# The second token half of x, also loaded transposed and scaled on chip, in one hybrid transformer layer

## The chip, the core and the metric

The kernel runs on one core of a Trainium2 chip. The core has a matrix engine, TensorE (PE; its weight loads are listed apart as PEld), three engines for elementwise work, VectorE (DVE), ScalarE (ACT) and GpSimd (POOL), and a queue engine, SyncE (SP), from which most transfers are issued. Each engine works through its own instruction stream; semaphores tie the streams together. The metric is the device time of one execution in microseconds.

## The reference

One layer is computed for 2048 tokens of width 1024, all in float32. The part that matters here is its beginning:

```python
u = rms_norm(h, g_mix_pre[l])          # x * rsqrt(mean(x*x) + eps) * g, per token
z = u @ w_in[l]                        # 1024 -> 2816 columns
qa, ka, va, qh, fh, ih, gh = jnp.split(z, IN_SPLITS, axis=-1)
```

The columns of z then feed a sliding-window attention (qa, ka, va) and a gated linear recurrence (qh, fh, ih, gh). For the recurrence the gate is f = lb + (1 - lb) sigmoid(fh), and running sums of log f over chunks of 64 tokens are exponentiated to give decays. Both outputs go through one projection, and cross-attention into 256 memory tokens and a SwiGLU network follow, each with its own norms.

## The kernel before

Every float32 operand of a matrix product is split into a high and a low part (`split2`), and a product is made of three matmuls, high by high, high by low and low by high (`products`, lines L1047, L1048 and L1049, which take turns). Large products are done in blocks with seven products in place of eight (`seven`); a block forms sums of weight tiles (`streamed`: sums at L1016, high parts at L911 on ScalarE or L913 on GpSimd, low parts at L914 on VectorE), multiplies, and copies banks of PSUM into `part` tiles on ScalarE (L1062) before it adds them up on VectorE (L571).

A planner in the framework orders the instructions of each engine ahead of time; the Python code is generators that the stage steps in turn, and a `yield` says how far a piece of work is moved behind the products. `behind()` ties an instruction to the last one of ScalarE and VectorE that `mark()` noted.

The first stage, `in_first`, lasts until about 268 us. It computes z for the first token half (1024 tokens) in eleven blocks of two 128-column groups, in the order `ORDER`: columns (4,5), (0,1), (2,3), then four forget-gate blocks (10+h, 6+h), then (14,15), (16,17), (18,19), (20,21). A block of the `seven` kind is 84 matmuls of 512 columns. Each has a closing generator, `after` in `in_block`. For a forget-gate block it runs `decays`: Ln (L652, with a table load before it and another before the next activation that needs the old table), two scans on VectorE (L656), small steps and a subtraction on GpSimd (L660, L661, L662, L665, L669), and exponentials on ScalarE (L668, L670, L672, L673). The gates themselves are tanh on ScalarE (L577) and a scale on GpSimd (L579); the other gates are L583 on ScalarE and L584 on VectorE.

Beside the blocks, the same stage prepares the second token half for the second stage. Block i gets some of the eight row tiles of x (`beside`): the tile is loaded on SP's queue into a `pair` tile when the block's weights are streamed; at the block's close `normed` squares it on ScalarE (L433), makes the factor 1/rms on GpSimd (`rstd`, L105 and L107) and scales the rows by factor and gain on VectorE (L435). After some yields eight transposes on TensorE (L1299) and two copies on ScalarE (L1300) turn it, and it is stored to a DRAM tile `un_d`. In the last blocks `fetch` loads `un_d` back in four pieces, and after all blocks the pieces are split into high and low parts (ScalarE L911, VectorE L914), ready for the second stage, whose first weights (`raw`) are split into `whi` on GpSimd (L148) and `wlo` on VectorE (L149), and whose first matmuls are L166, L167 and L168.

At the start of the stage the first half's own rows are squared, scaled and transposed too (L464, copies L470 on ScalarE, L481, L482), and the parts u of its second quarter are split on GpSimd (L913).

Of the kernel before, what the change touches and what calls it, by code (L numbers as in the profile page):

```python
# [24 lines left out]
KT = D // P  # L25
NFF = DFF // P
NB = 2
TB = T // NB
NPB = TB // P
# [19 lines left out]
class Layer:  # L49
# [27 lines left out]
    def store(self, dst, src):  # L77
        self.nc.sync.dma_start(dst, src)

    def put(self, dst, src):  # L80
        self.nc.scalar.dma_start(dst, src)

# [10 lines left out]
        self.load(g, ap[0:1, :].broadcast_to([P, D]))  # L93
        return g

    def rstd(self, parts, n, role):
# [9 lines left out]
        r = self.small(role + "_r")  # L106
        nc.gpsimd.tensor_tensor(r, v, self.mhalf[:, 0:1], ALU.pow)  # L107
        return r

# [61 lines left out]
    def run(self):  # L171
        tc, nc, I = self.tc, self.nc, self.I
        self._n = 0
        kw = dict(reuse_waits="tile")
        self.z_d = tc.dram_tile([DIN, T], F32, name="z_d")
        self.y_d = tc.dram_tile([NT, P, KT, P], F32, name="y_d")
        self.un_d = tc.dram_tile([KT, P, TB], F32, name="un_d")
# [247 lines left out]

    def pair_tile(self):
        self._n += 1
        return self.st_pool.tile([P, 2, D], F32, tag="pair", name=f"pair_{self._n}", bufs=5)

    def normed(self, x, junk):  # L430
        nc = self.nc
# [5 lines left out]
    def in_first(self):  # L437
# [59 lines left out]
                T[key[q, s]] = self.big.tile([P, 2, 4, 512], F32R, tag="big", name=f"u0_{q}{s}")  # L497
        second = {}

        def fetch():  # L500
            for s in range(2):
                for q in range(2):
                    r = self.pair_tile().rearrange("p a d -> p (a d)").rearrange("p (k t) -> p k t", k=4)
                    self.load(r, self.un_d[4 * q:4 * q + 4, :, s * 512:(s + 1) * 512].rearrange("k p t -> p k t"))
                    second[q, s] = r
                    yield

        beside = [(), (0,), (1, 2), (3,), (4,), (5,), (6,), (7,), (), (), ()]
        get = fetch()
        blocks = [("q" if i == 0 else "p" if i < 2 else "o",)  # L510
                  + self.in_block(*p, beside[i], get if i > 9 else (), None if i else lambda: x_loads(0, (2, 3)))
                  for i, p in enumerate(self.ORDER)]
        phases = self.phases([(lambda i, j, a, n: raw[i, j][:, a:a + n, :], 4, blocks, None, {})], T)
        next(phases)
        x_loads(1, range(4))
        b0 = first(0, "sh")
# [11 lines left out]
        self.mix_consts()  # L528
        for _ in phases:
            pass  # L530
        for _ in get:
            pass
        u = []
        for s in range(2):
            u.append([])
            for q in range(2):
                self._n += 1
                t = self.big.tile([P, 2, 4, 512], F32R, tag="big", name=f"u1_{q}{s}")
                r = second[q, s]
                for k in (0, 2):  # L540
                    self.split2(r[:, k:k + 2], t[:, 0, k:k + 2], t[:, 1, k:k + 2], "A")
                u[s] += [(t[:, 0, k, :], t[:, 1, k, :]) for k in range(4)]
        return u

    def in_block(self, ca, cb, beside, get, between):

        nc, w = self.nc, self.I["w_in"]
        z, x = [], []

        def load(t, j):  # L550
            if between and j:
                between()
            for i, c in enumerate((ca, cb)):
                self.load(t[:, i, :], w[c, :, j * 512:(j + 1) * 512])

        def stream(kind):
            for n in beside:
                t = self.pair_tile()
                self.load(t[:, 0, :], self.I["x"][TB + n * P:TB + (n + 1) * P, :])
                x.append((n, t))  # L560
            for _ in range(3):
                next(iter(get), None)
            return self.streamed(load, 4, kind, tiled=True)

        def out(i, j, a, b):
            if not z:
                z.append(self.pair_tile())
            c0 = (ca, cb)[i] * P
            zs = z[0][:, i, j * 512:(j + 1) * 512]
            if b is not None:  # L570
                nc.vector.tensor_tensor(zs, a, b, ALU.add)  # L571
                a = zs
            if c0 < C_QH or C_IH <= c0 < C_GH:
                if b is None:
                    nc.scalar.activation(zs, a, AF.Copy)
            elif C_FH <= c0 < C_IH:
                nc.scalar.activation(zs, a, AF.Tanh, scale=0.5)  # L577
                h = (c0 - C_FH) // P
                nc.gpsimd.tensor_scalar(zs, zs, self.fb[:, h:h + 1], self.fa[:, h:h + 1], ALU.mult, ALU.add)  # L579
            else:  # L580
                self._n += 1
                t = self.st_pool.tile([P, 512], F32, tag="part", name=f"th_{self._n}", bufs=self.parts)
                nc.scalar.activation(t, a, AF.Tanh, scale=0.5)  # L583
                nc.vector.scalar_tensor_tensor(zs, t, 1.0, a, ALU.add, ALU.mult)  # L584
# [63 lines left out]
    def decays(self, b, h, f, e1, e2):  # L648

        nc = self.nc  # L650
        NCB = TB // 64
        nc.scalar.activation(e1, f, AF.Ln)  # L652
        yield
        for s in range(TB // 512):
# [318 lines left out]
    @contextlib.contextmanager  # L973
    def behind(self):

        with contextlib.ExitStack() as at:
            for e in (mybir.EngineType.Activation, mybir.EngineType.DVE):
                if self.last.get(e) is not None:
                    at.enter_context(self.tc.issue_after(self.last[e]))
            yield  # L980

    def mark(self):

        traced = self.nc.cur_bb.bb.instructions
        self.last = {}
        for e in (mybir.EngineType.Activation, mybir.EngineType.DVE):
# [721 lines left out]
```

## Time and profile before

| | |
|---|---|
| median of 3 runs | 2575.55 us (2574.43 to 2576.95) |
| profiled execution | 2576.83 us |
| its span | 2574.7 us |
| TensorE busy | 2518.1 us, 98% |
| VectorE, ScalarE, GpSimd busy | 68%, 49%, 19% |
| matmuls on TensorE | 12160 recorded |

The span is the time between the first and the last instruction of the profiled execution. In the rows of the profile a line number such as L1299 is a line of the kernel, a group is written out<-in with the names of the program's tiles, and a bracket such as [0.93 <-POOL u L913] says how long the engine was idle before that instruction and what ended the wait. The waits of an engine are listed as total in us, number of times, longest. The clock column of the stretches is the share of TensorE's full clock that was granted.

### The profile page before, as it was taken

The page shows a single profiled execution, that of the slowest core. Times are in us where ns is not written, and L with a number is a line of the kernel's source. Part 1 is how long each engine was busy: PE and PEld are TensorE (multiplying, and loading weights), DVE is VectorE, ACT ScalarE, POOL GpSimd, SP SyncE. Part 2 cuts the span into 40 slices and gives each one's busy share as a digit, 9 for nine tenths or more (in the row PEclk, how much of TensorE's full clock was granted, in tenths as well). Part 3 has the DMA queues.
Part 4 walks back from the last instruction along what each step waited for, and adds up shares of the span by engine and source line. Part 5 has one row for each costly group of instructions (what it writes and reads, how often), then busy time and mean ns, then how long its engine had stood idle before and what let it go on. Part 6 is the DMA issues. An engine that isn't in the chain of part 4 may idle for free.

```text
span 2574.7 us, 34494 instructions
## 1 busy us (share of the span) xinstructions
PE 2518.1 (98%) x12160; PEld 2108.6 (82%) x12160; DVE 1747.3 (68%) x2781; ACT 1262.3 (49%) x2641; POOL 481.6 (19%) x651
## 2 busy tenths in 40 slices
PE   7989999999999999999999999999999999999998
PEld 6878788878997888888788888888888888888786
DVE  7675578778666668697776665575666566664756
ACT  5453366656555575565564333353333334543443
POOL 4240334321321334224210000000000000000022
PEclk9999999999999999999999999999999999999999
DMA  5335655484896787767983542253555434576798
GB/s 188 135 119 180 198 159 153 150 259 169 251 331 236 229 273 218 246 229 207 314 264 123 171 163 83 82 196 123 180 200 193 158 128 142 191 220 185 224 222 211
DMA packets 285389, 495.78 MB, mean 193 GB/s; under 512 B 20640, under 2 KB 143520, under 8 KB 285216
## 3 DMA queue, kind: packets, MB, share of 16 engines
q1 hardware_dynamic: 272256, 446.38, 51.5%
q0 software_dynamic: 10656, 38.80, 8.1%
q10 hardware_dynamic: 2304, 8.39, 0.8%
q8 instruction: 96, 1.57, 0.3%
q14 instruction: 77, 0.63, 0.1%
HBM read 326.78 MB, written 166.72 MB: 192 GB/s over the span
## 4 chain that ended last, share of the span: by engine, by line
PE 86%; DMA 5%; DVE 4%; issue 2%; POOL 2%; ACT 1%; SPq 0%; DVEq 0%; POOLq 0%; ACTq 0%
PE psm L1047 23%; PE psm L1049 23%; PE psm L1048 23%; PE psg L168 2%; PE psg L166 2%; PE psg L167 2%; PE pss L1299 2%; DMA pair<-in_x_dram 1%; PE pss L167 0%; PE psh L168 0%; PE psh L167 0%; PE pss L168 0%; PE pss L166 0%; PE psh L166 0%; DMA qd<-z_d 0%
## 5 line engine op out<-in xcount | busy, mean ns | idle before, releaser
L1047 PE MATMUL psm<-T,S 128*128 128x512 f32 x2664 | 1032.7, 392 | 14.9 <-ACT part L1062 8.6
L1048 PE MATMUL psm<-T,S 128*128 128x512 f32 x2664 | 1039.5, 390 | 0.0
L1049 PE MATMUL psm<-T,S 128*128 128x512 f32 x2664 | 1033.6, 391 | 2.2 <-DVE S L914 2.2
L1047 PEld LDWEIGHTS psm<-T,S 128*128 128x128 f32 x2664 | 501.1, 188 | 121.9 <-ACT part L1062 10.5
L1049 PEld LDWEIGHTS psm<-T,S 128*128 128x128 f32 x2664 | 500.9, 188 | 108.2 <-DVE S L914 4.4
L1048 PEld LDWEIGHTS psm<-T,S 128*128 128x128 f32 x2664 | 501.2, 188 | 102.6
L911 ACT ACTIVATE S<-sum 128x512 fp32r<-128x512 f32 (+1 forms) x338 | 207.9, 619 | 329.6 <-PE psm L1049 320.5
L914 DVE TENSOR_TENSOR S<-sraw,S 128x512 fp32r<-128x512 f32 (+1 forms) x311 | 214.8, 698 | 220.6 <-ACT S L911 208.3
L914 DVE TENSOR_TENSOR S<-sum,S 128x512 fp32r<-128x512 f32 (+1 forms) x404 | 277.1, 691 | 79.9 <-ACT S L911 67.0
L1062 ACT ACTIVATE part<-psm 128x512 f32<-128x512 f32 x297 | 175.3, 592 | 188.9 <-PE psm L1049 180.5
L911 ACT ACTIVATE S<-sraw 128x512 fp32r<-128x512 f32 (+1 forms) x272 | 166.4, 617 | 143.3 <-PE psm L1049 137.6
L1417 POOL DMA_DIRECT2D row<-y_d x28 | 25.0, 892 | 1071.4 <-DMA sraw<-hid_d 905.3
L1388 ACT ACTIVATE junk<-row 128x512 f32<-128x512 f32 x160 | 99.6, 624 | 95.3 <-DVE row L1410 34.6
L914 DVE TENSOR_TENSOR T<-row,T 128x1024 fp32r<-128x1024 f32 x104 | 123.3, 1193 | 29.6 <-ACT T L911 29.3
L166 PE MATMUL psg<-u,whi 128*128 128x512 f32 x352 | 141.8, 403 | 1.0 <-POOL whi L148 1.0
L168 PE MATMUL psg<-u,wlo 128*128 128x512 f32 x352 | 140.2, 398 | 1.5 <-DVE wlo L149 1.5
L167 PE MATMUL psg<-u,whi 128*128 128x512 f32 x352 | 140.1, 398 | 0.0
L911 ACT ACTIVATE T<-row 128x1024 fp32r<-128x1024 f32 x104 | 105.6, 1026 | 24.7 <-DMA row<-in_w_down_dram 11.8
L913 POOL TENSOR_SCALAR S<-sum 128x512 fp32r<-128x512 f32 x66 | 51.9, 787 | 217.8 <-PE psm L1049 138.6
L1592 DVE TENSOR_TENSOR part<-psm,part 128x512 f32<-128x512 f32 x66 | 45.5, 689 | 66.5 <-PE psm L1049 66.4
L149 DVE TENSOR_TENSOR wlo<-raw,whi 128x1024 fp32r<-128x1024 f32 x54 | 68.8, 1274 | 27.6 <-ACT whi L146 18.9
L1583 DVE TENSOR_TENSOR row<-psm,part 128x512 f32<-128x512 f32 x66 | 45.5, 690 | 56.0 <-PE psm L1049 55.7
(331 smaller groups left out, 3659.2 us busy)
## 6 DMA issues: line engine op xcount, KB each, us to landing
sraw<-in_w_gate_dram SPq DMA_DIRECT2D x44, 512.0 KB, 4.9
sraw<-in_w_up_dram SPq DMA_DIRECT2D x44, 512.0 KB, 4.8
hid_d<-row SPq DMA_DIRECT2D x44, 512.0 KB, 2.7
h_d<-row SPq DMA_DIRECT2D x32, 512.0 KB, 6.9
y_d<-row SPq DMA_DIRECT2D x32, 512.0 KB, 3.8
sraw<-hid_d SPq DMA_DIRECT2D x32, 512.0 KB, 5.2
row<-h_d POOLq DMA_DIRECT2D x30, 512.0 KB, 7.7
row<-y_d POOLq DMA_DIRECT2D x28, 512.0 KB, 7.2
```

Source lines behind the costliest of these rows:

```text
L149: nc.vector.tensor_tensor(lo, raw, f32(hi), ALU.subtract)
L166: nc.tensor.matmul(ps, ah, bh, start=(i == 0), stop=False)
L167: nc.tensor.matmul(ps, ah, bl, start=False, stop=False)
L168: nc.tensor.matmul(ps, al, bh, start=False, stop=(i == n - 1))
L911: self.nc.scalar.activation(hi, raw, AF.Copy)
L913: self.nc.gpsimd.tensor_scalar(hi, raw, 1.0, 1.0, ALU.mult, ALU.mult)
L914: self.nc.vector.tensor_tensor(lo, raw, f32(hi), ALU.subtract)
L1047: nc.tensor.matmul(ps, s[:, 0, k, :], t[:, 0, k, :], start=st, stop=False, **kw)
L1048: nc.tensor.matmul(ps, s[:, 0, k, :], t[:, 1, k, :], start=False, stop=False, **kw)
L1049: nc.tensor.matmul(ps, s[:, 1, k, :], t[:, 0, k, :], start=False, stop=sp, **kw)
L1062: nc.scalar.activation(t, ps, AF.Copy)
L1388: self.nc.scalar.activation(junk, a, AF.Square, scale=float(D) ** -0.5, accum_out=to)
```

## The change

Four things change, all in the first stage.

1. The host hands over the second half of x also transposed (`x_t`, four pieces of 1 MB) and the gain as columns (`g_mix_t`). `fetch` loads the pieces straight from there, from the eighth block on in program order, and not from `un_d`, which goes away with its stores, its row scaling (L435), its 64 transposes (L1299) and its copies (L1300).
2. The row tiles are still loaded and squared, to get the factors. They now go through a buffer of their own, `xr`, which exists once; the square overwrites the tile, and the factor goes to a column of `r_u`. The load is issued in the block's closing generator.
3. A new generator `scaled`, stepped beside the ninth block, spreads the factors: for each 512 tokens four transposes of a factor column broadcast to 128 x 128 give a PSUM bank whose every row holds the factors, and eight products on VectorE multiply pieces of `x_t` by gain column and bank, in place. A generator `parted`, beside the last block, splits the pieces into high and low parts. Both are tied with `behind()`, which now also holds an instruction behind the last one of TensorE.
4. `decays` has one more `yield` ahead of Ln, the other generators' yields change by one, `pair` tiles exist six times and not five, and the stores of z for columns from 18 on go out from GpSimd's queue (`store_late`).

```diff
+    def store_late(self, dst, src):
+        self.nc.gpsimd.dma_start(dst, src)
...
-        return self.st_pool.tile([P, 2, D], F32, tag="pair", name=f"pair_{self._n}", bufs=5)
+        return self.st_pool.tile([P, 2, D], F32, tag="pair", name=f"pair_{self._n}", bufs=6)
...
         def fetch():
+            self.load(g_t, I["g_mix_t"])
             for s in range(2):
                 for q in range(2):
...
-                    self.load(r, self.un_d[4 * q:4 * q + 4, :, s * 512:(s + 1) * 512].rearrange("k p t -> p k t"))
+                    self.load(r, I["x_t"][2 * s + q])
...
-        beside = [(), (0,), (1, 2), (3,), (4,), (5,), (6,), (7,), (), (), ()]
+        def scaled():
+            for s in range(2):
+                ps = self.bank("sh"[s])
+                with self.behind():
+                    for i in range(4):
+                        n = 4 * s + i
+                        nc.tensor.transpose(ps[:, i * P:(i + 1) * P], self.r_u[:, n:n + 1].broadcast_to([P, P]),
+                                            self.ident)
+                for q in range(2):
+                    r = second[q, s]
+                    for k in range(4):
+                        with self.behind():
+                            nc.vector.scalar_tensor_tensor(r[:, k, :], r[:, k, :], g_t[:, 4 * q + k:4 * q + k + 1],
+                                                           ps, ALU.mult, ALU.mult)
+                        yield
+
+        def parted():
+            for n in (1, 3, 2, 0):
+                for _ in range(n):
+                    yield
+                s, q = divmod(sum(map(len, u)) // 4, 2)
...
+                with self.behind() if n else contextlib.nullcontext():
+                    for k in (0, 2):
+                        self.split2(second[q, s][:, k:k + 2], t[:, 0, k:k + 2], t[:, 1, k:k + 2], "A")
+                u[s] += [(t[:, 0, k, :], t[:, 1, k, :]) for k in range(4)]
+
+        beside = [(), (0, 1), (2, 3), (4,), (5,), (6,), (7,), (), (), (), ()]
...
-                  + self.in_block(*p, beside[i], get if i > 9 else (), None if i else lambda: x_loads(0, (2, 3)))
+                  + self.in_block(*p, beside[i], get if i > 6 else (), None if i else lambda: x_loads(0, (2, 3)))
...
-        phases = self.phases([(lambda i, j, a, n: raw[i, j][:, a:a + n, :], 4, blocks, None, {})], T)
+        phases = self.phases([(lambda i, j, a, n: raw[i, j][:, a:a + n, :], 4, blocks, None, {8: [scaled], 10: [parted]})], T)
...
         def after():
-            for n, p in x:
-                self.normed(p[:, 0, :], p[:, 1, :])
+            def rows(n):
+                self._n += 1
+                t = self.st_pool.tile([P, D], F32, tag="xr", name=f"xr_{self._n}", bufs=1)
+                self.load(t, self.I["x"][TB + n * P:TB + (n + 1) * P, :])
+                return t
+
+            t = rows(beside[0]) if beside else None
...
-                self.store(self.z_d[c * P:(c + 1) * P, 0:TB], z[0][:, i, :])
-            for _ in range(1 if C_FH <= c0 < C_IH else 4):
-                yield
-            for n, p in x:
-                self.store_transposed(self.un_d, n, self.transposed(p[:, 0, :], p[:, 1, :]))
+                (self.store if c < 18 else self.store_late)(self.z_d[c * P:(c + 1) * P, 0:TB], z[0][:, i, :])
+            for _ in range(1 if C_FH <= c0 < C_IH else 3):
+                yield
+            for n in beside:
+                if n != beside[0]:
+                    t = rows(n)
+                    for _ in range(3):
+                        yield
+                ss = self.small("n_s")
+                nc.scalar.activation(t, t, AF.Square, accum_out=ss)
+                self.rstd([ss], D, "n", self.r_u[:, n:n + 1])
                 yield
...
         NCB = TB // 64
+        yield
         nc.scalar.activation(e1, f, AF.Ln)
...
-            for e in (mybir.EngineType.Activation, mybir.EngineType.DVE):
+            for e in (mybir.EngineType.Activation, mybir.EngineType.DVE, mybir.EngineType.PE):
```

In the planner's order that results, the eight squares all stand among ScalarE's instructions of the first 20 to 57 us of the old timeline, because nothing holds their loads back; of the eight transposes four stand within the first products of the ninth block and four in the tenth block.

More of the change, by code (lines that the diff above doesn't have):

```diff
@@ L94, in gain, with rstd @@
         return g
-    def rstd(self, parts, n, role):
+    def rstd(self, parts, n, role, r=None):
         nc = self.nc
@@ L105, in rstd @@
             nc.gpsimd.tensor_scalar(v, parts[0], 1.0 / n, EPS, ALU.mult, ALU.add)
-        r = self.small(role + "_r")
+        if r is None:
+            r = self.small(role + "_r")
         nc.gpsimd.tensor_tensor(r, v, self.mhalf[:, 0:1], ALU.pow)
@@ L176, in run @@
         self.y_d = tc.dram_tile([NT, P, KT, P], F32, name="y_d")
-        self.un_d = tc.dram_tile([KT, P, TB], F32, name="un_d")
         self.h1t_d = tc.dram_tile([NT, P, KT, P], F32, name="h1t_d")
@@ L498, in in_first @@
         second = {}
+        self.r_u = self.mc.tile([P, NPB], F32, name="r_u")
+        g_t = self.mc.tile([P, KT], F32, name="g_t")
+        u = [[], []]
         def fetch():
+            self.load(g_t, I["g_mix_t"])
             for s in range(2):
@@ new lines, in parted @@
+        def parted():
[4 more added lines that the diff above has]
+                self._n += 1
+                t = self.big.tile([P, 2, 4, 512], F32R, tag="big", name=f"u1_{q}{s}")
+                with self.behind() if n else contextlib.nullcontext():
+                    for k in (0, 2):
+                        self.split2(second[q, s][:, k:k + 2], t[:, 0, k:k + 2], t[:, 1, k:k + 2], "A")
+                u[s] += [(t[:, 0, k, :], t[:, 1, k, :]) for k in range(4)]
@@ L530, in in_first @@
             pass
[L531 to L542, printed above, removed]
         return u
@@ L547, in in_block @@
         nc, w = self.nc, self.I["w_in"]
-        z, x = [], []
+        z = []
         def load(t, j):
@@ L556, in stream @@
         def stream(kind):
[L557 to L561, printed above, removed]
+            for _ in range(2):
                 next(iter(get), None)
@@ L586, in after @@
         def after():
-            for n, p in x:
-                self.normed(p[:, 0, :], p[:, 1, :])
+            def rows(n):
+                self._n += 1
+                t = self.st_pool.tile([P, D], F32, tag="xr", name=f"xr_{self._n}", bufs=1)
+                self.load(t, self.I["x"][TB + n * P:TB + (n + 1) * P, :])
+                return t
+            t = rows(beside[0]) if beside else None
             c0 = ca * P
@@ L985, in mark @@
         self.last = {}
-        for e in (mybir.EngineType.Activation, mybir.EngineType.DVE):
+        for e in (mybir.EngineType.Activation, mybir.EngineType.DVE, mybir.EngineType.PE):
             self.last[e] = next((i for i in reversed(traced) if i.engine == e), None)
@@ L1699 @@
             host[name] = tiled(host[name].T if name == "wq_x" else host[name])
+    host["x_t"] = np.ascontiguousarray(host["x"][TB:].reshape(2, 512, 2, 4, P).transpose(0, 2, 4, 3, 1)).reshape(4, P, 4, 512)
+    host["g_mix_t"] = np.ascontiguousarray(host["g_mix_pre"].reshape(KT, P).T)
     nc = _bacc.Bacc("TRN2", target_bir_lowering=False, num_devices=1, dynamic_dma_scratch_size=2048)
```

## The prediction

> **What bounds the kernel now.** The page comes first: its busy shares and its costliest groups.
>
> ```profile
> PE 2518.1 (98%) x12160; PEld 2108.6 (82%) x12160; DVE 1747.3 (68%) x2781; ACT 1262.3 (49%) x2641; POOL 481.6 (19%) x651
> ...
> L1047 PE MATMUL psm<-T,S 128*128 128x512 f32 x2664 | 1032.7, 392 | 14.9 <-ACT part L1062 8.6
> ```
>
> TensorE is busy 98% of the span, so only two things can move the time: work taken off PE, and pauses of PE. The diff touches the first stage (0 to about 268 us), which alone holds nearly all of the 8.6 us that PE waited for L1062. The waits of PE there, then busy time by stretches, with the granted clock in the column after the five engines:
>
> ```profile
> PE psm L1047 <- ACT part L1062: 8.1, 4, 4.9
> ...
> PE psg L168 <- DVE wlo L149: 1.5, 1, 1.5
> PE psg L166 <- POOL whi L148: 1.0, 1, 1.0
> PE psm L1047 <- POOL u L913: 0.9, 1, 0.9
> PE psm L1047 <- ACT S L911: 0.8, 1, 0.8
> ```
>
> ```profile
> 20.00:40.00 20.00, 16.24 (x130) 14.83 (x130) 14.64 (x19) 12.09 (x24) 11.08 (x17) 1.00 0.20 73
> ...
> 120.00:140.00 20.00, 19.74 (x92) 16.17 (x90) 14.84 (x20) 11.68 (x19) 9.95 (x12) 1.00 0.50 159
> ...
> 160.00:180.00 20.00, 15.09 (x60) 12.07 (x60) 16.62 (x20) 12.88 (x20) 10.35 (x11) 0.83 0.42 149
> ...
> 260.00:280.00 20.00, 16.99 (x67) 13.05 (x66) 15.96 (x20) 6.46 (x10) 14.46 (x13) 0.91 0.90 297
> ```
>
> The four waits for L1062 stand at the starts of the forget-gate blocks (two of them long). In 160:180 the clock averages 0.83: 0.17 x 20 / 0.5 = 6.8 us at half clock, of which about 5.5 us lie after PE resumed, so 2.75 us more are lost there. In 260:280 it is 0.91: 3.6 us at half clock, 1.6 to 1.8 us lost. Who makes L1062 late is read from ScalarE's timeline (idle time before an instruction, and its releaser, in brackets) and from the chain of waits:
>
> ```profile
> 132.92 1.06 ACT L433 ACTIVATE pair<-pair 128x1024 f32<-128x1024 f32 x1 [4.27 <-DMA pair<-in_x_dram]
> ...
> 139.31 1.28 ACT L583 ACT_TABLE_LOAD   x1
> ...
> 157.55 1.06 ACT L433 ACTIVATE pair<-pair 128x1024 f32<-128x1024 f32 x1 [4.09 <-DMA pair<-in_x_dram]
> ...
> 163.40 1.06 ACT L652 ACTIVATE pair<-pair 128x1024 f32<-128x1024 f32 x1 [1.83 <-POOL pair L579]
> ```
>
> ```profile
> 119.51 0.50 PE L1047 MATMUL psm<-T,S 128*128 128x512 f32 x1 [0.74 <-ACT part L1062]
> ...
> 141.74 0.50 PE L1047 MATMUL psm<-T,S 128*128 128x512 f32 x1 [2.00 <-ACT part L1062]
> ...
> 166.90 0.80 PE L1047 MATMUL psm<-T,S 128*128 128x512 f32 x1 [4.91 <-ACT part L1062]
> ```
>
> ```profile
> 78.01 0.88 PE pss L1299 x8
> ...
> 126.89 5.95 DMA pair<-in_x_dram
> ...
> 150.48 6.99 DMA pair<-in_x_dram
> ...
> 201.64 0.45 PE psm L1047 x2
> ...
> 207.77 0.87 PE pss L1299 x8
> ```
>
> ScalarE works through its queue in order. The square of a row tile of x (L433) stands there ahead of the gate's activations; its load, 6 to 7 us long, came late; behind it came th, L577, the table load, Ln (after POOL's L579), a second table load, L583, and only then L1062, for which PE waited.
>
> **The change, part by part.**
>
> *Transposes.* Of eight sets of eight at L1299 seven lie on PE's path at 0.87 us (two are in the chain above). The first set, at 37.55 us, ends in the wait for POOL's u (the 0.9 row) and costs nothing. The new kernel has eight transposes in all, tied to PE's own order: 0.87. Net 7 x 0.87 - 0.87 = **5.2 us gained**. The two copies of each set and L435 leave ScalarE and VectorE; the sixteen new products of x, gain and factor go to VectorE:
>
> ```profile
> 119.94 0.68 DVE L584 SCALAR_TENSOR_TENSOR pair<-th,psm 128x512 f32<-128x512 f32 x1
> ```
>
> Sixteen at that price are 11 us, spread over blocks 8 to 10, about 60 us in which VectorE was busy some 10 us in 20. Costed at nothing; without that cover each of them ahead of a PE operand would cost up to 0.68.
>
> *Squares away from the gate blocks.* All eight now stand early (20 to 57 us). In the second gate block the square held ScalarE's queue for 4.27 + 1.06; without it L577 still has to await VectorE's sum, about 1.5 of that, so the second table load ends near 136.8 instead of 140.6 (139.31 + 1.28). PE paused at 139.74 there, and L583 and L1062 take 1.1: 2 us of slack. What stays is inherent: L583 reads the last product of the old block, then L1062 (0.5 + 0.6 us) frees a bank, and PE has only three matmuls of 0.227 (the 0.45 of two, above) between: 1.1 + 0.2 - 0.68, about 0.65 us a boundary, much as the first of the three waits (0.74) and the fourth of the table (8.1 - 0.74 - 2.00 - 4.91, about 0.5). At the last gate boundary the order moved differently: L670, L668, L672 and L673, which wait for POOL's L661 and L665, now stand ahead of L583 and L1062. Their timing at that place before:
>
> ```profile
> 180.65 1.06 ACT L652 ACTIVATE pair<-pair 128x1024 f32<-128x1024 f32 x1
> ...
> 189.00 1.06 ACT L670 ACTIVATE pair<-pair 128x1024 f32<-128x1024 f32 x1 [4.25 <-POOL pair L661]
> ...
> 192.11 1.07 ACT L1062 ACTIVATE part<-psm 128x512 f32<-128x512 f32 x2
> ```
>
> ```profile
> 181.44 0.69 DVE L1016 TENSOR_TENSOR sum<-sraw,sraw 128x512 f32<-128x512 f32 x1 [2.10 <-DMA sraw<-in_w_in_dram]
> ...
> 182.65 2.33 DVE L656 TENSOR_TENSOR_SCAN pair<-reset,pair 128x512 f32<-128x512 f32 x2
> ```
>
> ```profile
> 180.78 0.39 PE L1047 MATMUL psm<-u,S 128*128 128x512 f32 x1
> ```
>
> The scans will not stand behind a sum that waits for weights, as at 181.44, but follow Ln at 181.7: with what lay between scan and L670 (182.65 to 189.00, less a POOL product of 1.05) L670 starts about 187; the exponentials, L583 and L1062 take 4.2 more with POOL's last small steps: 191.3. PE, whose new order comes back to that bank 36 matmuls after the block's start (180.78 + 36 x 0.227 = 188.95), waits about **2.5 us**. Before: 0.74 + 2.00 + 4.91 + 2.75 (clock) + 0.84 (the wait for L911, at the last boundary) + a 0.2 next to it = 11.4. After: 3 x 0.65 + 2.5 = 4.45. **7.0 us gained.** Bounds: nothing waits at the last boundary, 9.5; or the 2.5 us pause also halves the clock as the 4.9 one did, 4.2.
>
> *The early squares.* They share one buffer, so load and square alternate, and each square stands in ScalarE's order among the copies L470 that feed the first 512-wide matmuls:
>
> ```profile
> 36.90 1.09 ACT L470 ACTIVATE pair<-pss 128x512 f32<-128x512 f32 x2 [0.26 <-PE pss L464]
> ```
>
> ```profile
> 39.62 0.96 PE L1047 MATMUL psm<-u,S 128*128 128x512 f32 x3 [0.93 <-POOL u L913]
> ```
>
> The price of a load: the one row tile loaded with little beside it took from 61.79 to about 65, the median of all eight is 5.6.
>
> ```profile
> 61.79 0.33 SPq L75 DMA_DIRECT2D pair<-in_x_dram  x1
> ...
> 65.08 1.06 ACT L433 ACTIVATE pair<-pair 128x1024 f32<-128x1024 f32 x1 [2.05 <-DMA pair<-in_x_dram]
> ```
>
> ```profile
> pair<-in_x_dram SPq DMA_DIRECT2D x8, 512.0 KB, 5.6
> ```
>
> In 20:40 the DMA share was 0.20 and SP's queue holds nothing but these loads (and one of g_mem), so I take 3.2 plus a square of 1.06. The second square can end about 30.7 (behind the copies of that time); the third then stands at 34.0 to 35.1, the fourth at 38.3 to 39.4, so the last copies move from 36.90 to 39.4; POOL's u follows, interleaved with two factors of r_u, and the first 512-wide matmul comes at about 41.5 instead of 39.62: **1.9 us lost**. PE has only sixteen transposes, 1.7 us, in the seven before 41.5. Around the stage's last pauses (1.0 and 1.5 us, a few matmuls between) the clock fell; here I expect the same, one stretch of that length, **1.7 lost**. Bounds 0 and 5: no delay, or two such stretches (3.4) with 1.6. The Trainium skill (TensorE: Matmul & The Clock Gate, "What's actually happening") says that the clock halves after an idle window of about 3.4 us, in windows that run freely. Read strictly, no such window would be quite idle here, the clock would hold and the time be 2564.3; this trace's 0.91 in 260:280 followed pauses with matmuls between, which speaks against the strict reading. The later squares delay copies that have 2 us and more to spare; costed at nothing. If the loads took 5.6, the fourth square would end at 45.6 instead of 39.4, and with two stretches at half clock 1.9 + 6.2 + 3.4 = 11.5 would be lost instead of 3.6.
>
> *The end of the stage.*
>
> ```profile
> 260.73 1.28 SPq L75 DMA_DIRECT2D raw<-in_w_in_dram  x3
> ...
> 264.15 1.40 POOL L148 TENSOR_SCALAR whi<-raw 128x1024 fp32r<-128x1024 f32 x1 [13.91 <-DMA raw<-in_w_in_dram]
> ...
> 264.57 2.13 DVE L584 SCALAR_TENSOR_TENSOR pair<-th,pair 128x512 f32<-128x512 f32 x2
> ...
> 266.62 1.21 DVE L149 TENSOR_TENSOR wlo<-raw,whi 128x1024 fp32r<-128x1024 f32 x1
> ```
>
> The raw load is still tied to the same matmul, 15 before the stage's last, so the pause of 1.0 for whi stays. The splits (parted) begin inside the last block, and L149 need not stand behind two L584: about **1.0 us gained**, between 0 (the raw load sets all) and 2.6 (the clock holds too). SP loses sixteen row transfers of x and un_d and gains eight earlier ones; the four x_t loads, as large as the four of un_d that they replace, go out three blocks before their use. The last four z_d stores move from SP to POOL's queue, nearest row:
>
> ```profile
> L1417 POOL DMA_DIRECT2D row<-y_d x28 | 25.0, 892 | 1071.4 <-DMA sraw<-hid_d 905.3
> ```
>
> Two of them (0.9 each) stand ahead of whi on POOL, but their data are ready some 10 us before: nothing, or at worst 1.8 late. The rest of the program keeps its order but for a few neighbours: 0.
>
> *Sum.* 5.2 + 7.0 - 3.6 + 1.0 = 9.6. The profiled execution took 2576.83 us (span 2574.7 and 2.1 around it), 1.28 above the median of 2575.55. 2576.83 - 9.6 = 2567.2; against the median 2565.95, so I forecast **2566 us**.
>
> **Rivals.**
>
> *Half of it comes back.* The 2.5 us pause halves the clock (2.75) and the early stretch costs 5: 5.2 + 4.2 - 5 + 0 = 4.4, 2571. For it: the page's 0.83 after one pause. Against it: the second L1062 pause of 2.00 us lies in 120:140, where the clock stayed at 1.00. Loads at 5.6 us would give 9.6 - 7.9 = 1.7, 2574, in the same class.
>
> *Slower: Ln goes on holding L1062 back.* Ln and its two table loads still stand ahead of L583 and L1062 at the other three boundaries. Were L579 or the scan's neighbours on POOL late there by more than the 2 us of slack, each would cost as the last: 2.5 + 2.75 instead of 0.65, 3 x 4.6 = 13.8, and 2.75 at the last: 9.6 - 16.6 = -7.0, 2582.5. It decides the sign from an average of about 2.5 us a boundary for all four. For it: the row at 163.40, where Ln waited 1.83 for L579. Against it: that L579 followed an L577 which the late square had pushed.
>
> *More.* The early copies hide the squares, the last boundary waits for nothing, the clock holds at the end: 5.2 + 9.5 + 0 + 2.6 = 17.3, 2558.
>
> *It does nothing at the end of the stage*: the raw load sets that end alone, 2567; it lies inside the forecast.
>
> **How the numbers follow.** A measurement here tells 0.2% (5.15 us) from no change: faster is under 2570.4, slower over 2580.7. Forecast (2562 to 2570.4) 0.50; more gain 0.15; half, contended loads included, 0.20; slower 0.10; 0.05 lies between half and slower. So faster 0.65, same 0.25, slower 0.10. The range 2559 to 2576 leaves out about 0.05 below and 0.13 above.
>
> **What would show it.** L1299 gone and eight transposes in its place; the L1062 waits in the first stage at about 4.5 us in four, none over 3, and the clock 1.00 in 160:180; the first 512-wide matmul at 41 to 42 us, with a clock under 1.00 in 20:60; L149's wait under 1. The prediction is wrong if PE waits for ScalarE at the gate boundaries as long as before, if the row loads take 5 us or more, or if new waits of PE on VectorE show in blocks 8 to 10.

## The result, and the profile after

The changed kernel takes 2581.25 us (median of 9 runs, 2579.5 to 2587.34) against 2576.3 us before: a ratio of 1.0021 [1.0012, 1.003]. It is 5 us slower, where 2566 us, 10 us faster, was forecast. The profiled execution took 2584.18 us with a span of 2582.4, 7.7 us above that of the kernel before.

Lines have moved, most by some thirty: L1047 is now L1079, L1062 is L1094, L1299 is L1331, L148 and L149 are L152 and L153, L166 to L168 are L170 to L172. First the page, the busy shares and the costliest group:

```profile
PE 2522.1 (98%) x12104; PEld 2103.4 (81%) x12104; DVE 1742.3 (67%) x2789; ACT 1256.5 (49%) x2625; POOL 471.4 (18%) x655
...
L1079 PE MATMUL psm<-T,S 128*128 128x512 f32 x2664 | 1031.7, 391 | 13.1 <-ACT S L943 5.8
```

56 fewer matmuls are recorded, and yet PE is busy 4.0 us longer (2518.1 before). That is the first sign that the loss is more than a new wait. The waits of PE in the first 300 us of the changed kernel:

```profile
PE psm L1079 <- ACT part L1094: 4.1, 5, 1.8
...
PE psm L1079 <- POOL u L945: 3.0, 1, 3.0
...
PE psg L170 <- ACT z L659: 1.6, 1, 1.6
PE psg L172 <- DVE wlo L153: 1.5, 1, 1.5
PE psg L170 <- POOL whi L152: 0.7, 1, 0.7
```

The wait for L1094 (L1062 before) halved, 8.1 to 4.1. Its pieces, the first 512-wide matmul and the first product of the next stage, from PE's timeline:

```profile
41.99 1.42 PE L1079 MATMUL psm<-u,S 128*128 128x512 f32 x3 [2.98 <-POOL u L945]
...
122.25 0.50 PE L1079 MATMUL psm<-T,S 128*128 128x512 f32 x1 [0.48 <-ACT part L1094]
...
142.66 0.50 PE L1079 MATMUL psm<-T,S 128*128 128x512 f32 x1 [0.71 <-ACT part L1094]
...
163.10 0.50 PE L1079 MATMUL psm<-T,S 128*128 128x512 f32 x1 [0.71 <-ACT part L1094]
...
184.97 0.50 PE L1079 MATMUL psm<-T,S 128*128 128x512 f32 x1 [1.75 <-ACT part L1094]
...
244.90 0.50 PE L1079 MATMUL psm<-T,S 128*128 128x512 f32 x1 [0.49 <-ACT part L1094]
...
260.41 0.50 PE L170 MATMUL psg<-u,whi 128*128 128x512 f32 x1 [0.71 <-POOL whi L152]
```

The same product of the kernel before:

```profile
265.61 0.50 PE L166 MATMUL psg<-u,whi 128*128 128x512 f32 x1 [1.04 <-POOL whi L148]
```

So the first stage, where all four terms of the forecast lie, ended 5.2 us earlier, and what follows it took 12.9 us longer than before. Part of that are waits late in the program, which the change doesn't touch. Behind 794 us PE waited for S:

```profile
PE psm L1079 <- ACT S L943: 5.8, 3, 2.5
PE psm L1081 <- DVE S L946: 4.9, 5, 1.5
```

Before, the same two were 3.7 and 2.2. A profile is one execution, and these waits differ between the profiles of all kernels below. The other part of the loss shows where PE waits for nothing. Two stretches of the second stage's first products without a pause, first and last row of each, before and after:

```profile
286.62 0.39 PE L168 MATMUL psg<-u,wlo 128*128 128x512 f32 x1
...
290.92 0.39 PE L166 MATMUL psg<-u,whi 128*128 128x512 f32 x1
```

```profile
282.74 0.39 PE L172 MATMUL psg<-u,wlo 128*128 128x512 f32 x1
...
286.94 0.40 PE L172 MATMUL psg<-u,wlo 128*128 128x512 f32 x1
```

Before, 19 steps took 4.30 us, 226 ns each; after, 18 steps took 4.20 us, 233 ns each: the same instruction, at full clock, 7 ns slower. (Over all steps of 215 to 245 ns between 260 and 500 us the mean goes from 229.1 to 233.4.) The first stage shows the same in the durations (minimum, median and maximum in ns, first and last start) of its products with u, before and after:

```profile
L1048 PE MATMUL psm<-u,S x125: 387/389/397, 60.2 to 257.1; 128*128 128x512 f32 x125
```

```profile
L1080 PE MATMUL psm<-u,S x132: 393/394/398, 60.4 to 255.6; 128*128 128x512 f32 x132
```

No instruction of these products was changed. What the change did alter is the place of their operands: `r_u` and `g_t`, two tiles of 32 bytes in each partition, come first in pool `mc`, and all tiles allocated behind them in it, among them the weights S, whi and wlo, moved by 64 bytes, while u stayed where it was in pool `big`. In the compiled programs' addresses, taken modulo 256 bytes, the moving and the stationary operand of a 512-wide product before had the same start in 9640 of 9736 cases. After, 1632 products with an operand that stayed and one that moved have starts 64 apart; 324 products T x S, with both moved, agree. 1632 times 5 ns (by the durations) or 7 ns (by the starts) is 8 to 11 us. By the mean steps it is 8.4: 4.3 ns for the 900 products of 512 columns in the first stage (227.2 and 231.5, in the table below) and as much for the 1056 of the second.

### The profile page after: what moved, and what is told of

It reads as the page before. It is cut to its first block, busy times and chain, and to the rows that moved or that the text cites. A ratio compares the mean times of both kernels' runs of the same rounds, so it can differ in the third digit from the quotient of the medians.

```text
span 2582.4 us, 34329 instructions
## 1 busy us (share of the span) xinstructions
PE 2522.1 (98%) x12104; PEld 2103.4 (81%) x12104; DVE 1742.3 (67%) x2789; ACT 1256.5 (49%) x2625; POOL 471.4 (18%) x655
## 4 chain that ended last, share of the span: by engine, by line
PE 80%; DMA 7%; DVE 5%; issue 4%; POOL 2%; ACT 2%; SPq 0%; DVEq 0%; POOLq 0%; ACTq 0%
PE psm L1079 21%; PE psm L1081 21%; PE psm L1080 21%; PE psg L170 2%; PE psg L171 2%; PE psg L172 2%; PE pss L1331 1%; DMA u_d<-row 1%; DMA row<-d_s 1%; DVE S L946 1%; DVE T L946 1%; DMA row<-in_x_dram 1%; DMA sraw<-in_w_in_dram 1%; DMA qd<-z_d 1%; ACT junk L1420 0%
## 5 line engine op out<-in xcount | busy, mean ns | idle before, releaser
L1079 PE MATMUL psm<-T,S 128*128 128x512 f32 x2664 | 1031.7, 391 | 13.1 <-ACT S L943 5.8
L1079 PEld LDWEIGHTS psm<-T,S 128*128 128x128 f32 x2664 | 500.6, 188 | 121.6 <-ACT part L1094 7.9
L1094 ACT ACTIVATE part<-psm 128x512 f32<-128x512 f32 x297 | 175.8, 593 | 188.4 <-PE psm L1081 180.9
L170 PE MATMUL psg<-u,whi 128*128 128x512 f32 x352 | 143.0, 406 | 2.3 <-ACT z L659 1.6
L172 PE MATMUL psg<-u,wlo 128*128 128x512 f32 x352 | 140.9, 400 | 1.5 <-DVE wlo L153 1.5
L153 DVE TENSOR_TENSOR wlo<-raw,whi 128x1024 fp32r<-128x1024 f32 x54 | 68.2, 1263 | 22.9 <-ACT whi L150 20.0
```

The lines of the kernel that those rows point to most:

```text
L153: nc.vector.tensor_tensor(lo, raw, f32(hi), ALU.subtract)
L170: nc.tensor.matmul(ps, ah, bh, start=(i == 0), stop=False)
L172: nc.tensor.matmul(ps, al, bh, start=False, stop=(i == n - 1))
L1079: nc.tensor.matmul(ps, s[:, 0, k, :], t[:, 0, k, :], start=st, stop=False, **kw)
L1094: nc.scalar.activation(t, ps, AF.Copy)
```

## The experiments

The theory: a 512-wide product is slower when the starts of its two operands in a partition differ by something that is no multiple of some size; this costs the changed kernel about 10 us and has nothing to do with what the change computes. The rival: the loss is in the change's own work, with its early row loads or with neighbours that moved, and the pitch is a symptom.

**Addresses, first batch.** The change with 64 bytes more in front, so that the tiles are moved by 128 in all:

```diff
-        g_t = self.mc.tile([P, KT], F32, name="g_t")
+        g_t = self.mc.tile([P, KT + 16], F32, name="g_t")[:, :KT]
```

> The changed kernel with 64 unused bytes behind the tile g_t, so that all tiles behind r_u and g_t lie 128 bytes, and not 64, further than before; the order of instructions on every engine stays. Theory A (the two small tiles moved the stationary operands S, whi and wlo of the first two stages to an address that differs by 64 bytes from the moving operands modulo 128, and each such 512-wide matmul starts 6 ns later: 1632 of them, some 9.7 us): the pitch in the first two stages goes back from 233 to 227 ns, and the time to about 2571.5 us. Rival B (the slower pitch comes from the work that the change adds beside the matmuls, transfers or the queue of GpSimd): 233 ns and 2581 us stay.

And the kernel before, with nothing but 64, 32 or 128 bytes of unused space ahead of the same tiles:

```diff
-        self.fa = ph.tile([P, 4], F32, name="fa")
+        self.fa = ph.tile([P, 20], F32, name="fa")[:, :4]
```

(12 and 36 in place of 20 for the other two.)

> The kernel before with one small tile (fa) 64 bytes larger, nothing else. Theory A: the 512-wide matmuls of the first two stages go from 227 to 233 ns, the time from 2576 to about 2586 us. Rival B: no difference.

> The kernel before with fa 32 bytes larger. If theory A holds for any difference of the two addresses modulo 128, as e2: 233 ns and 2586 us. If only the half of the 128 bytes counts (addresses 32 and 64 modulo 128 lie in different halves), the same 233; if only a difference of 64 exactly counts, 227 ns and 2576 us. Rival B: no difference.

> The kernel before with fa 128 bytes larger, as a control: theory A 227 ns and 2576 us, since the addresses agree modulo 128 again; a theory in which any shift of the tiles costs time (other banks, other neighbours) gives some us more.

Measured, against the kernel before on the same chip (2578.84 us): the change moved by 128, 1.001 [0.9999, 1.0021]; before plus 64, 1.0031 [1.0021, 1.0041]; plus 32, 1.0022 [1.0011, 1.0032]; plus 128, 1.0012 [1.0002, 1.0022]. The first stage's products with u in the kernel before plus 64:

```profile
L1048 PE MATMUL psm<-u,S x126: 388/394/398, 59.9 to 257.4; 128*128 128x512 f32 x126
```

Unused bytes alone make the old kernel 8 us slower and turn its 389 ns into 394, so the theory holds and the rival doesn't explain the pitch. 128 bytes, which I had taken for agreement in the first of these runs, is none.

**Second batch.** 512 bytes in all for the change, and 256 and 512 for the kernel before:

```diff
-        g_t = self.mc.tile([P, KT], F32, name="g_t")
+        g_t = self.mc.tile([P, KT + 112], F32, name="g_t")[:, :KT]
```

> The changed kernel with 448 unused bytes behind g_t: all tiles behind r_u and g_t lie 512 bytes further than before. Theory A2 (the pitch is 227 ns only where the stationary and the moving operand agree modulo 512 bytes; a shift of 128 was no agreement): 227 ns in the first two stages where the changed kernel had 233, 1632 x 6 ns, some 9 to 10 us, so 0.9965 of the changed kernel's time and about 0.998 to 0.999 of the kernel before. Rival B (the work that the change adds slows the matmuls): 231 to 233 ns stay, and 1.001 to 1.002.

> The kernel before with fa 256 bytes larger. If the operands need to agree modulo 512: pitch 229 to 233 ns on average in the first two stages, 4 to 9 us slower. If modulo 256: 227 ns, no difference.

> The kernel before with fa 512 bytes larger, the control: theory A2 227 ns and no difference in time. If any shift costs: 229 to 233 ns and 4 us or more.

Measured: the change 0.9982 [0.9973, 0.999], 2575.48 against 2578.94 us; before plus 256, 0.9997 [0.9988, 1.0006]; plus 512, 1.0003 [0.9994, 1.0012]. The products with u, of the change with 512 and of the kernel before plus 256:

```profile
L1080 PE MATMUL psm<-u,S x132: 388/389/389, 59.7 to 252.5; 128*128 128x512 f32 x132
```

```profile
L1048 PE MATMUL psm<-u,S x126: 389/389/397, 60.2 to 259.4; 128*128 128x512 f32 x126
```

So starts that agree modulo 256 are enough, and the change, freed of the shift, is faster than before by 0.2%. From 1.0021 to 0.9982 is 0.39%, 10 us: what the shift cost (6 to 15 between the ends of the two intervals).

**Relative or absolute.** The kernel before with 64 bytes more in the first pool of all, so that both operands move:

```diff
-                nc.gpsimd.memset(pool.tile([P, 24], F32, name="pad"), 0.0)
+                nc.gpsimd.memset(pool.tile([P, 40 if pool is self.cst else 24], F32, name="pad"), 0.0)
```

> The kernel before with the unused tile pad of the outermost pool 64 bytes larger, so that the moving operands and the stationary ones of all stages move by the same 64 bytes. Theory A2 (only the difference of the two addresses modulo 256 counts): 227 ns and no difference in time, where 64 bytes on the stationary side alone cost 0.3%. Rival (the absolute address counts): 231 to 233 ns in some stage, 5 us or more.

Measured 1.0011 [0.9999, 1.0022], with the products at the old duration:

```profile
L1048 PE MATMUL psm<-u,S x125: 387/389/397, 60.1 to 257.2; 128*128 128x512 f32 x125
```

The interval reaches both sides of nothing, so the time alone doesn't settle it; the duration does: the relation of the two starts counts, and not where they are. All the address runs together; the mean step from one 512-wide matmul to the next was taken over steps of 215 to 245 ns between 60 and 260 us:

```
kernel               starts mod 256 of the 1632 products   mean step   time ratio
                     (moving, stationary)                  ns
before               160, 160                              227.2       1
before + 256         160, 160                              227.1       0.9997
before + 512         160, 160                              227.1       1.0003
before, all + 64     224, 224                              227.1       1.0011
before + 32          160, 192                              231.6       1.0022
before + 64          160, 224                              231.6       1.0031
before + 128         160,  32                              231.1       1.0012
change               160, 224                              231.5       1.0021
change, 128 in all   160,  32                              231.1       1.0010
change, 512 in all   160, 160                              227.1       0.9982
```

**The squares.** What is left of the change without the shift? The early squares had delayed the first 512-wide matmul by 2.3 us and the clock had halved there, so the next run holds each square behind TensorE's last instruction in the planned order, on top of the 512 bytes:

```diff
-                nc.scalar.activation(t, t, AF.Square, accum_out=ss)
+                with self.behind():
+                    nc.scalar.activation(t, t, AF.Square, accum_out=ss)
```

> As the run before, and each early square is tied behind the last instructions of ScalarE, VectorE and TensorE at its step (as the products of scaled are), so that the squares no longer stand ahead of the copies L470. Theory C (the early squares cost about 2.4 us of waiting ahead of the first 512-wide matmul and two stretches at half clock, 3.4 us): the first 512-wide matmul back at 39.5 to 40 us instead of 42, no half clock before 60 us, 4 to 6 us less than the run before. Rival: the squares, back at the gate blocks, hold L1062 up there again, and the gain is 2 us or less.

Measured 0.9987 [0.9978, 0.9995], 2575.53 us: no gain over 2575.48. The first 512-wide matmul and the waits for ScalarE's `part`, and two stretches, the early one and that of the last gate boundary (clock in the column after the five engines):

```profile
39.18 0.96 PE L1080 MATMUL psm<-u,S 128*128 128x512 f32 x3 [1.83 <-POOL u L946]
```

```profile
PE psm L1080 <- ACT part L1095: 7.5, 5, 3.0
```

```profile
40.00:60.00 20.00, 20.00 (x90) 16.56 (x89) 19.97 (x21) 8.52 (x10) 2.06 (x3) 1.00 0.30 105
...
180.00:200.00 20.00, 19.35 (x80) 15.84 (x81) 13.28 (x21) 4.49 (x10) 2.98 (x4) 0.91 0.44 157
```

The early stretch was won (39.18 and not 41.95), and the gate blocks lost it again: the squares stood there in front of the gate's activations, 7.5 us of waits for 4.4, and the last pause, 2.99, was followed by a half clock. So the next run puts three squares beside the second block, one beside the third and four beside the seventh, still held behind TensorE. In its trace the first four start between 82 and 109 us, ahead of the first gate boundary, and the other four between 199 and 221 us, behind the last:

```diff
-        beside = [(), (0, 1), (2, 3), (4,), (5,), (6,), (7,), (), (), (), ()]
+        beside = [(), (0, 1, 2), (3,), (), (), (), (4, 5, 6, 7), (), (), (), ()]
...
-                    for _ in range(3):
+                    for _ in range(2):
```

> The changed kernel with the 448 unused bytes, the squares tied to their step as in the run with late squares, and the row tiles moved away from the middle gate blocks: three beside the second block, one beside the third, four beside the seventh. Theory C with both halves (early squares cost some 6 us at the start, squares in the gate blocks cost 1 us a boundary, some 3 to 4 us in all, where they are loaded in time): the first 512-wide matmul at 39 to 40 us, L1062's line waits 0.5 to 0.8 at the second and third gate boundary and 2 at the last, no half clock before 180 us; 3 to 5 us less than the aligned change, about 0.9965 of the kernel before. Rival (what is saved in the first stage is given back later): the time of the aligned change, 0.998.

Measured 0.9978 [0.9967, 0.9988], 2571.5 against 2578.12 us, faster than both kernels. Its first 512-wide matmul, the stage's end, its waits, and the early stretch:

```profile
39.28 0.96 PE L1080 MATMUL psm<-u,S 128*128 128x512 f32 x3 [1.83 <-POOL u L946]
...
256.14 0.50 PE L170 MATMUL psg<-u,whi 128*128 128x512 f32 x1 [1.90 <-POOL whi L152]
```

```profile
PE psm L1080 <- ACT part L1095: 4.4, 5, 1.9
```

```profile
40.00:60.00 20.00, 20.00 (x83) 16.38 (x82) 19.45 (x20) 8.52 (x10) 5.32 (x3) 0.91 0.30 104
```

Both gains stand here at once: 39.28 and 4.4 us. The half clock in 40:60, which the expectation had not, stayed. The stage ends 9.5 us earlier than before. That this beats the 0.9982 of the change with 512 bytes isn't shown, the intervals overlap; so the rival, that the gain of the stage is given back later, isn't ruled out.

**The transposes alone.** The kernel before without the 64 transposes and their copies:

```diff
-                self.store_transposed(self.un_d, n, self.transposed(p[:, 0, :], p[:, 1, :]))
+                self.store_transposed(self.un_d, n, p[:, 0, :].rearrange("p (k t) -> p k t", k=KT))
```

> The kernel before without the 64 transposes of the second half and their 16 copies: the scaled rows are stored as they are, which leaves the turning of the second token half out of the computation. It measures the term of the transposes alone. Theory (seven sets of 0.87 us lay on the path): 6 us less, 0.9975 of the kernel before, the pauses for L1062 as they were. Rival (their time only filled pauses, or is given back in the later stages): 2 us or less.

Measured 1.0021 [1.001, 1.0031], 2583.89 against 2578.12 us: slower by 5 us, with 64 transposes gone from PE; neither the theory nor the rival had that. Waits, the two long pauses, and the stretches with them:

```profile
PE psm L1047 <- ACT part L1062: 14.5, 5, 6.2
```

```profile
144.26 0.80 PE L1047 MATMUL psm<-T,S 128*128 128x512 f32 x1 [6.21 <-ACT part L1062]
...
191.43 0.80 PE L1047 MATMUL psm<-T,S 128*128 128x512 f32 x1 [5.10 <-ACT part L1062]
```

```profile
140.00:160.00 20.00, 15.74 (x60) 12.86 (x61) 12.81 (x17) 9.31 (x17) 5.84 (x9) 0.83 0.40 134
...
180.00:200.00 20.00, 14.90 (x55) 11.76 (x55) 13.10 (x16) 8.23 (x14) 5.93 (x7) 0.83 0.22 79
```

With the row loads and squares still at the gate blocks, PE got there sooner and waited longer, 14.5 us for 8.1, and two stretches of 6.8 us at half clock (0.17 x 20 / 0.5) came with them where before had one. The transposes had filled time in which PE would have waited. In this profile the stage ends at 267.33, 1.7 us later than before; the rest of the 5 us lies behind it, and what it is this run doesn't show. The transposes' 5.2 us is no gain by itself.

## Why the prediction was wrong

**The step that failed** is the last sentence of the part on the stage's end: "The rest of the program keeps its order but for a few neighbours: 0". The order was kept. But the sum took the step of the 512-wide products (0.227) as given, and read from the diff only which instructions come and go. Two new tiles of 32 bytes, ahead of all others in their pool, moved the weights against u, and 1632 products of the first two stages became 4 to 7 ns longer: 8.4 us by the steps, about 10 by the medians, in the place of 0. None of the rivals had it, so the range didn't hold the time; that the slower rival's 2582.5 lies near it is chance, since the waits of that rival didn't come. A hint was in the code: the kernel allocates tiles named `pad` and never reads them.

**Without it** the change gives 0.9982, 4.6 us [2.6, 7.0] of 2579, and not 9.6: faster, on the forecast's side. The rival in which half comes back has nearly this number, 4.4, but not by what happened: its pause at the last gate boundary, 1.95 us here, halved no clock. Term by term, in the changed kernel's profile and in that of the change with 512 bytes, of which these are the first 512-wide matmul, the last gate boundary and the stage's end, then the stretches of its start:

```profile
41.95 1.65 PE L1079 MATMUL psm<-u,S 128*128 128x512 f32 x3 [2.77 <-POOL u L945]
...
183.09 0.50 PE L1079 MATMUL psm<-T,S 128*128 128x512 f32 x1 [1.95 <-ACT part L1094]
...
258.47 0.50 PE L170 MATMUL psg<-u,whi 128*128 128x512 f32 x1 [1.91 <-POOL whi L152]
```

```profile
20.00:40.00 20.00, 16.23 (x125) 15.01 (x123) 12.54 (x18) 14.60 (x29) 11.21 (x20) 0.95 0.54 177
40.00:60.00 20.00, 18.05 (x74) 14.87 (x75) 18.66 (x20) 13.52 (x20) 12.97 (x14) 0.88 0.46 160
```

*Gate blocks*: right. Forecast 0.65 three times and 2.5; measured 0.48, 0.71, 0.71 and 1.75 in the changed kernel, 3.65 in all for 4.45. The fifth wait, 0.49 at 244.90, is no gate block's: it is the fourth of the kernel before (0.50 at 249.97), which the prediction took for one of a gate block; neither of its sums has it. The clock stayed whole in 160:180, as forecast. The slower rival, with Ln holding L1062 back at each boundary, didn't come.

*Transposes*: the eight new ones cost little, by the first row below; but the 5.2 us is only to be had together with the gate blocks' term. I had costed the two one by one, and the run without transposes gave a loss. The groups of the changed kernel, the row loads of its squares (KB, median us) behind them:

```profile
L522 PE MATMUL pss<-ident,r_u 128*128 128x128 f32 x8 | 1.2, 272 | 0.0
```

```profile
L528 DVE SCALAR_TENSOR_TENSOR pair<-pair,g_t,pss 128x512 f32<-128x512 f32 x16 | 11.3, 741 | 1.5 <-PE pss L522 1.5
```

```profile
xr<-in_x_dram SPq DMA_DIRECT2D x8, 512.0 KB, 3.2
```

*Early squares*: right, and the size within a microsecond. The loads took 3.2 us as assumed. GpSimd's timeline in the changed kernel has the two small factors between the two pieces of u, as the forecast said:

```profile
37.90 1.90 POOL L945 TENSOR_SCALAR u<-pair 128x512 fp32r<-128x512 f32 x2
40.03 0.35 POOL L108 TENSOR_SCALAR n_v<-n_s 128x1 f32<-128x1 f32 x1 [0.24 <-ACT xr L632]
40.46 0.87 POOL L111 TENSOR_TENSOR r_u<-n_v,mhalf 128x1 f32<-128x1 f32 x1
41.32 1.20 POOL L945 TENSOR_SCALAR u<-pair 128x512 fp32r<-128x512 f32 x2
```

The first 512-wide matmul came at 41.99 (forecast 41.5): 2.4 lost, not 1.9. The clock halved twice, not once; the stretches of the changed kernel:

```profile
20.00:40.00 20.00, 15.73 (x119) 14.68 (x117) 12.17 (x17) 14.36 (x29) 11.10 (x19) 0.91 0.54 177
40.00:60.00 20.00, 18.01 (x71) 14.37 (x72) 18.93 (x20) 13.59 (x20) 11.68 (x14) 0.91 0.45 158
...
160.00:180.00 20.00, 19.15 (x82) 14.94 (x81) 16.95 (x21) 12.00 (x18) 8.65 (x11) 1.00 0.56 202
...
260.00:280.00 20.00, 17.33 (x72) 13.38 (x72) 15.57 (x16) 5.13 (x7) 15.74 (x15) 1.00 0.78 246
```

0.09 x 20 / 0.5 is 3.6 us at half clock in each of the first two (3.41 by the trace's record of the clock). Only the second, from 42.28 on, comes on top. The first shows in the duration of PE's 256-wide products:

```profile
27.15 0.38 PE L1080 MATMUL psm<-u,S 128*128 128x256 f32 x1 [2.61 <-DVE u L485]
...
28.52 0.31 PE L1079 MATMUL psm<-u,S 128*128 128x256 f32 x1
28.63 0.41 PE L1080 MATMUL psm<-u,S 128*128 128x256 f32 x1
```

It lies ahead of the first 512-wide matmul, so that what it cost is inside the 2.4 already, and it follows a wait for VectorE that the kernel before has too (2.19). In all 2.4 + 1.7 = 4.1 were lost where the forecast has 3.6. With 512 bytes the clock was at half from 38.04 to 44.87, 2.9 us of it behind the first 512-wide matmul: 2.3 + 1.5 = 3.8.

*End of the stage*: gained about 2.1 for 1.0 in the changed kernel, but by the clock, which held in 260:280 (1.8), and 0.3 by the two waits (2.2 for 2.5); L153's wait stayed 1.5 where under 1 was said. With 512 bytes the waits turned round, 1.9 for whi and 0.5 for wlo, 2.4 in all, and the clock fell as before: about 0.1. In the changed kernel wlo (261.35) came behind two splits of u on VectorE; with 512 bytes VectorE waited 0.94 for GpSimd's whi, which had taken 1.91 us and not 1.40.

With 512 bytes the stage thus ended at 258.47 for 265.61, 7.1 us earlier, and the terms add to 6.9: 6.4 from the gate blocks (11.4 less 0.50, 0.72, 0.72, 1.95 and a wait of 1.09 for VectorE's S at 164.98), 5.2 from the transposes, 3.8 lost to the squares and 0.9 to the longer wait for whi. In the changed kernel the same sum is 7.75 + 5.2 - 4.1 + 0.3 = 9.2, and 5.2 were measured. The 4.0 between are the shift's share in this stage: 900 products at 4.3 ns are 3.9.

So without the shift the forecast's terms nearly hold up to the stage's end, but of the 7.1 us there the medians keep 4.6. The profile with 512 bytes is as a whole even longer than that of before (2576.4 for 2574.7; its execution was 2.7 above its median): up to the first product T x S behind the second stage (at 787 to 802 us in all runs) 5.6 us came back, with the clock at half for 17.1 us there and before for 6.8, and behind it 3.2. Half-clock stretches of the later stages come and go between executions (at 640:670 the clock is 0.94 in the profile of before and 0.89 in this one, in 780:810 it is 1.00 and 0.94). But the part behind that product took 1782.2 to 1786.3 us in the five profiles of the change and 1777.4 to 1783.3 in the seven of the kernel before with and without unused bytes. Some of the gain seems to be given back there; whether it is, and by what, no run shows.

## What to carry to other kernels

Before an edit that adds, drops or resizes a tile is priced by its instructions, compare the start addresses of both operands of the large matmuls in the two programs: here 64 bytes of unrelated tiles cost about twice what the edit gave, and the pitch of back-to-back matmuls in a stretch without waits shows it at once. Work taken off the busiest engine counts only if what that engine then waits for is moved too. And work moved off one engine's queue belongs where that engine has time, not at the next tight place: of three placings of the same eight squares only the one clear of both the start and the gate boundaries kept both gains within the first stage. And what a stage gains is not yet gained at the end of the program.

## What was not expected of the hardware

A 128x512 product in these kernels starts every 227 ns in the first stage's mean and every 229 in the second's if the two operands' starts in a partition agree modulo 256 bytes. If they differ by 32, 64 or 128, the mean step is about 4 ns longer in the first stage and 3 to 4 in the second (7 in the stretch shown for 64); moving both by 64 costs no duration. Other distances weren't tried, and why it is so no run shows.

The clock at TensorE halved in stretches of 3.4 or 6.8 us. In the changed kernel one began right behind a pause of 2.98 us; with the squares moved late, a pause of 1.83 at the same place had no such stretch, and one of 1.83 with the squares clear of both places had (0.91 in 40:60). The Trainium skill (TensorE: Matmul & The Clock Gate, "What's actually happening") has free-running windows of about 3.4 us, and a halving after an idle one. The lengths agree with it, and so does the phase: in the record of the clock of each of the thirteen traces all half-clock stretches start whole multiples of 3.413 us apart (in the changed kernel at 28.63, 42.28, 540.63, 653.27 and 796.63 us). A wholly idle window isn't needed: none of these pauses, 1.8 to 3.0 us, is as long as a window.

How much is needed can be read off, if each trace is cut into windows at these multiples and PE's idle time in each is added up from its rows (gaps over 60 ns, from 20 us on). At full clock, 57 windows were followed by a half clock, and PE was idle in them for 1.45 to 3.41 us; the other 9545 had at most 1.94. So the halving depends on how a pause falls on the windows. With the squares late, the pause of 1.83 us, up to 39.18, was cut in two by a boundary at 38.42; with the squares clear of both places, the one up to 39.28 lay wholly in the window from 37.24.
